# Merge weights of three attention groups: one set for both halves, and by token for the last head pair

## The chip, the cores and the metric

The kernel runs on one core of a Trainium2 chip. The metric is the device time of one execution in microseconds. The engines that matter here are TensorE (PE, and PEld for its weight loads), VectorE (DVE), ScalarE (ACT), GpSimd (POOL) and the queue of SyncE (SP), which issues nearly all DMAs.

## What is computed

The reference is a two-layer decoder trunk of 1024 tokens with width 1024: layer one has a forgetting attention and a gated ConvFFN, layer two a dilated attention with three groups of heads ("mixer B") and again a ConvFFN. The change lies in mixer B, where the outputs of the three groups are merged by softmax weights over their log-sum-exp:

```
for g, (window, dil) in enumerate(B_GROUPS):          # (128,1), (512,4), (2048,16)
    o_g, lse_g = dilated_branch(q[:, :, g], kv[:, :, 0, g], kv[:, :, 1, g], dil, slopes[g])
    outs.append(o_g)
    lses.append(lse_g)
alpha = softmax(stack(lses, axis=0), axis=0)
o = sum(alpha[..., None] * stack(outs, axis=0), axis=0)
x = x + o.reshape(B, S, B_OUT_WIDTH) @ b_w_out[bl]
```

There are 8 heads of 64 in each group, and each head has one weight per token and group.

## The kernel before

Matrix products are made of float32r pairs: each operand is split into a high part (ACT, `split` L152) and a low part (DVE, L153), and three matmuls (L116, L117, L118) stand for one product.

Mixer B works on 12 units: 4 head pairs p, and for each the groups g = 2, 1, 0 in this order. A unit's attention (`attend_b`) goes through two halves m of the tokens and two heads j; after both heads of a half it calls `each_half(m)`. While a unit attends, the projections of the next unit (values, queries, keys) are woven in as filler by `weave`. The last unit (p = 3, g = 0) has as filler the first half of the output projection (`out_proj(b_w_out[0], 0, xT)`), which may begin once the last pair's first half is placed in `yh` and `yl`. All instructions are then put in order by a scheduler with a timeline of its own: each engine's and each queue's order is fixed at build time, and an engine whose next instruction waits does not go past it.

The softmax leaves, for each token, head and group, the minimum (k = 0) and the sum (k = 1) in a tile `st` with tokens on the partitions. `spread` transposes a group's 32 columns on PE (L534), copies them out on ACT into the one-buffer tile `srow` (L537, L539) and sends them to DRAM (`stat_sp[p]`) in token order: for g = 0 in rows of 512 bytes (L543), for g = 1 in four DMAs of single 4-byte elements, 8 rows of 128 elements each (L548), for g = 2 in eight DMAs of 8-byte pieces (L554).

`group_weights` is called once per half. It loads the half's stats on 32 partitions with 32 tokens each (two DMAs, L563, tile `stats`), makes the three weights in 12 small DVE instructions and one Exp on ACT (L567 to L577), writes them to DRAM (L578, tile `wt`), and reads them back spread over 64 partitions per head (two DMAs, L581, tile `wb` of two buffers, 128 x 3 x 512). `merge_b` multiplies the groups' outputs `og` by them (L589: g = 2 and 1 on the given engine, g = 0 on DVE) and adds (L590, L591). `emit_o` splits the result and sends it to DRAM (`o_sp`, tiles `oh` and `ol` with one buffer each), or, for the last pair, splits it straight into `yh` and `yl`.

For the pairs 0 to 2 this is done in the next pair's g = 2 unit: the weights of both halves at `each_half(0)`, the products and sums at `each_half(1)` with POOL for g = 2 and 1. The tiles of `group_weights` have one buffer, so the second half's loads come after the first half's stats have been read. For the last pair, `each_half(m)` in its own g = 0 unit spreads that half's g = 0 stats, makes the weights and merges on DVE at once. Ahead of that unit `reload` brings back, half by half, the earlier pairs' outputs into `yh` and `yl` (L614, L615) and the residual into `xT` (L617).

Of the kernel before, what the change touches and what calls it, by code (L numbers as in the profile page):

```python
# [8 lines left out]
F32 = mybir.dt.float32  # L9
# [3 lines left out]
ALU = mybir.AluOpType  # L13
# [3 lines left out]
P = 128  # L17
# [33 lines left out]
def trunk(ctx, tc, x, a_w_in, a_b_f, a_w_out, b_w_q, b_w_out, kv_norm_g, w_kv,  # L51
# [478 lines left out]
    def spread(ap, psc, st, g, dst, ms=(0, 1)):  # L530

        n = 16 * len(ms)
        tp = psc.tile([P, H2], F32, name="sc")
        nc.tensor.transpose(tp[:n, :P], st[:, g, 16 * ms[0]:16 * ms[0] + n], ident)  # L534
        rows = ap.tile([32, P], F32, name="srow")
# [5 lines left out]
        if g == 0:  # L541
            for i, m in enumerate(ms):
                nc.sync.dma_start(dst[0, m].rearrange("k j (b t) -> (k j b) t", t=P),  # L543
                                  rows[16 * i:16 * i + 16])
# [13 lines left out]
    def group_weights(ap, src, dst, m):  # L558

        T = 32  # L560
        r = ap.tile([32, NG, 2, T], F32, name="stats")
        for k in range(2):
            nc.sync.dma_start(r[:, :, k], src[:, m, k].rearrange("g j (b t) -> (j b) g t", t=T))  # L563
        mn, sm = (ap.tile([32, T], F32, name=n) for n in ("mn", "sm"))
        e = ap.tile([32, NG, T], F32, name="ew")
        el = r[:, :, 1]
        nc.vector.tensor_tensor(out=mn, in0=r[:, 0, 0], in1=r[:, 1, 0], op=ALU.min)  # L567
        nc.vector.tensor_tensor(out=mn, in0=mn, in1=r[:, 2, 0], op=ALU.min)
        for g in range(NG):
            nc.vector.tensor_tensor(out=e[:, g], in0=r[:, g, 0], in1=mn, op=ALU.subtract)  # L570
        nc.scalar.activation(e, e, AF.Exp, scale=-1.0)
        nc.vector.tensor_tensor(out=el, in0=e, in1=el, op=ALU.mult)
        nc.vector.tensor_tensor(out=sm, in0=el[:, 0], in1=el[:, 1], op=ALU.add)
        nc.vector.tensor_tensor(out=sm, in0=sm, in1=el[:, 2], op=ALU.add)
# [3 lines left out]
        nc.sync.dma_start(dst[m].rearrange("g j (b t) -> (j b) g t", t=T), e)  # L578
        w = ap.tile([P, NG, H2], F32, name="wb", bufs=2)
        for j in range(2):  # L580
            nc.sync.dma_start(w[64 * j:64 * j + 64],  # L581
                              dst[m][:, j].unsqueeze(0).to_broadcast([64, NG, H2]))
        return w
# [782 lines left out]
```

## Time and profile before

| what | value |
|---|---|
| median of 3 runs | 2688.72 us (2683.15 to 2688.9) |
| profiled execution | 2687.51 us, of which the span is 2685.7 us |
| mean granted TensorE clock | 0.984 |
| PE busy | 2576.5 us (96% of the span) |
| DVE busy | 1953.0 us (73%) |
| ACT busy | 1334.9 us (50%) |
| POOL busy | 546.7 us (20%) |

The profiled execution is the one that all rows below come from, and a sum over its rows is made against its own 2687.51 us; what is outside its span is 1.8 us. Mixer B's attention takes the stretch from about 1380 to 1940 us of the span; the merges of the pairs 0, 1 and 2 fall around 1500 to 1535, 1640 to 1675 and 1780 to 1815 us, and that of the last pair into 1893 to 1940 us. In a windows row the columns give, for one stretch, the busy time of each engine with the number of its instructions, the granted TensorE clock as a share of its full speed, the DMA engines' busy share and what they moved. In a timeline row the bracket at the end says how long the engine stood idle before and what ended that.

### The profile page before, as it was taken

How to read it: one execution, taken by the hardware profiler on the slowest of the kernel's cores; microseconds unless marked ns; L12 is line 12 of the kernel's file. 1: busy time of each engine (PE TensorE's matmuls, PEld its weight loads, DVE VectorE, ACT ScalarE, POOL GpSimd, SP SyncE). 2: the span in 40 equal slices, each digit the busy share in tenths (PEclk: the TensorE clock that was granted, in tenths of full speed). 3: DMA queues.
4: the chain of work that ended last, by engine and by line, in shares of the span. 5: the costliest groups of instructions: out<-in, count | busy, mean ns of one | idle time of the engine just before them, and what ended most of it. 6: DMA issues, size and time to landing. Idle time of an engine off the chain costs nothing.

```text
span 2685.7 us, 36967 instructions
## 1 busy us (share of the span) xinstructions
PE 2576.5 (96%) x12734; PEld 2148.6 (80%) x12734; DVE 1953.0 (73%) x3859; ACT 1334.9 (50%) x2832; POOL 546.7 (20%) x629
## 2 busy tenths in 40 slices
PE   7999999999999999999899999999589999999998
PEld 5998888787788888888688787878467888888887
DVE  6677777767876777788866766666588777777787
ACT  6566555654544443444455555555345444443444
POOL 0222222310121121121132223231011221111121
PEclk9999999999999999999899999999799999999999
DMA  5122112532111111111413222233421111111113
GB/s 185 48 65 57 49 50 71 184 89 83 48 48 55 52 59 54 49 51 51 136 40 40 69 32 73 37 73 95 111 88 43 52 48 55 51 59 55 48 48 114
DMA packets 282467, 182.12 MB, mean 68 GB/s; under 512 B 40480, under 2 KB 259368, under 8 KB 282280
## 3 DMA queue, kind: packets, MB, share of 16 engines
q1 hardware_dynamic: 282168, 179.75, 24.2%
q8 instruction: 100, 1.64, 0.2%
q14 instruction: 87, 0.71, 0.1%
q10 hardware_dynamic: 112, 0.02, 0.0%
HBM read 151.55 MB, written 23.98 MB: 65 GB/s over the span
## 4 chain that ended last, share of the span: by engine, by line
PE 82%; DVE 9%; DMA 4%; ACT 3%; issue 2%; POOL 0%; SPq 0%; POOLq 0%; ACTq 0%; DVEq 0%
PE up L781 29%; PE mm L116 13%; PE mm L117 13%; PE mm L118 13%; PE po L247 4%; PE tp L234 3%; DVE u L732 1%; DVE t L257 1%; PE sc L357 1%; DMA wb<-wt 1%; PE sc L358 1%; PE up L116 1%; PE up L118 1%; PE up L117 1%; DVE pt L153 1%
## 5 line engine op out<-in xcount | busy, mean ns | idle before, releaser
L116 PE MATMUL mm<-yh,wh 128*128 128x512 f32 x960 | 383.7, 400 | 12.0 <-ACT yh L152 7.3
L117 PE MATMUL mm<-yl,wh 128*128 128x512 f32 x960 | 382.7, 399 | 3.9 <-DVE yl L153 3.4
L118 PE MATMUL mm<-yh,wl 128*128 128x512 f32 x960 | 380.6, 396 | 0.0
L152 ACT CAST wh<-wraw 128x512 fp32r<-128x512 f32 x228 | 140.8, 619 | 356.5 <-PE up L781 306.6
L886 DVE TENSOR_TENSOR xT<-mm,xT 128x512 f32<-128x512 f32 x320 | 217.8, 684 | 107.0 <-PE mm L118 105.3
L153 DVE TENSOR_TENSOR wl<-wraw,wh 128x512 fp32r<-128x512 f32 x228 | 169.4, 748 | 150.3 <-ACT wh L152 150.3
L781 PE MATMUL up<-yh,wh 128*128 128x512 f32 x704 | 274.4, 390 | 0.9 <-ACT wh L152 0.9
L781 PE MATMUL up<-yl,wh 128*128 128x512 f32 x704 | 274.1, 389 | 0.0
L781 PE MATMUL up<-yh,wl 128*128 128x512 f32 x704 | 268.9, 389 | 0.0
L117 PE MATMUL mm<-ml,wh 128*128 128x512 f32 x576 | 225.4, 391 | 1.4 <-DVE ml L153 1.4
L116 PE MATMUL mm<-mh,wh 128*128 128x512 f32 x576 | 224.7, 390 | 0.0
L118 PE MATMUL mm<-mh,wl 128*128 128x512 f32 x576 | 223.9, 389 | 0.0
L116 PEld LDWEIGHTS mm<-yh,wh 128*128 128x128 f32 x960 | 182.4, 190 | 51.4 <-ACT yh L152 7.9
L247 PE MATMUL po<-pt,v 128*128 128x256 f32 x1040 | 195.6, 294 | 19.8 <-DVE pt L153 14.7
L117 PEld LDWEIGHTS mm<-yl,wh 128*128 128x128 f32 x960 | 182.6, 190 | 37.3 <-DVE yl L153 4.1
L118 PEld LDWEIGHTS mm<-yh,wl 128*128 128x128 f32 x960 | 182.4, 190 | 34.6
L152 ACT CAST pt<-tp 128x128 fp32r<-128x128 f32 (+2 forms) x408 | 149.6, 382 | 104.6 <-PE tp L234 57.7
L153 DVE TENSOR_TENSOR pt<-tp,pt 128x128 fp32r<-128x128 f32 (+2 forms) x408 | 169.4, 432 | 44.0 <-ACT pt L152 39.3
L247 PEld LDWEIGHTS po<-pt,v 128*128 128x128 f32 x1040 | 156.8, 192 | 39.6 <-DVE pt L153 19.1
L765 POOL TENSOR_TENSOR sraw<-fraw 128x512 f32<-128x512 f32 x40 | 68.3, 1709 | 580.0 <-DMA fraw<-in_ffn_w_up_dram 314.4
L95 DVE TENSOR_TENSOR wl<-wraw,wh 128x512 fp32r<-128x512 f32 x176 | 127.0, 724 | 75.1 <-ACT wh L94 66.2
L781 PEld LDWEIGHTS up<-yh,wh 128*128 128x128 f32 x704 | 132.2, 188 | 29.8 <-ACT wh L152 1.8
(346 smaller groups left out, 6086.9 us busy)
## 6 DMA issues: line engine op xcount, KB each, us to landing
wraw<-in_ffn_w_down_dram SPq DMA_DIRECT2D x104, 256.0 KB
fraw<-in_ffn_w_up_dram SPq DMA_DIRECT2D x88, 256.0 KB
wraw<-in_ffn_w_up_dram SPq DMA_DIRECT2D x88, 256.0 KB
wraw<-in_a_w_in_dram SPq DMA_DIRECT2D x60, 256.0 KB
wraw<-in_w_kv_dram SPq DMA_DIRECT2D x48, 256.0 KB
wraw<-in_a_w_out_dram SPq DMA_DIRECT2D x32, 256.0 KB
xT<-x_sp SPq DMA_DIRECT2D x32, 256.0 KB
wraw<-in_b_w_q_dram SPq DMA_DIRECT2D x24, 256.0 KB
```

The lines of the kernel that those rows point to most:

```text
L95: nc.vector.tensor_tensor(out=wl, in0=raw, in1=wh.bitcast(F32), op=ALU.subtract)
L116: nc.tensor.matmul(ps, ah, bh, start=(i == 0), stop=False)
L117: nc.tensor.matmul(ps, ah, bl, start=False, stop=False)
L118: nc.tensor.matmul(ps, al, bh, start=False, stop=(i == n - 1))
L152: nc.scalar.copy(h, src)
L153: return nc.vector.tensor_tensor(out=l, in0=src, in1=h.bitcast(F32), op=ALU.subtract).ins
L234: nc.tensor.transpose(tp[:, i * P:(i + 1) * P], c, ident)
L247: nc.tensor.matmul(po[:, col:col + 2 * P], v(kb), pt[:, hl, i * 2 * P:(i + 1) * 2 * P], start=(first and i == 0 and hl == 0), stop=(last a ...
L257: nc.vector.tensor_tensor_reduce(out=t[:, a:b], in0=sc, in1=m, scale=1.0, scalar=INIT if ci == 0 else nm[ci - 1], op0=ALU.add, op1=ALU.min ...
L765: nc.gpsimd.tensor_tensor(out=raw[n], in0=raw[a], in1=raw[b], op=op)
L781: nc.tensor.matmul(ps[bank], a[:, c], b[:, k], start=(start and k == 0 and i == 0), stop=(k == KH - 1 and i == 2), skip_group_check=True)
L886: nc.vector.tensor_tensor(out=xT[:, d, sl], in0=ps, in1=xT[:, d, sl], op=ALU.add)
```

## The change

Pairs 0 to 2: `group_weights` takes both halves at once. It loads their stats on 64 partitions (four DMAs), makes the weights once (`weigh`, which has 14 DVE instructions, and one Exp), writes them with two DMAs, and issues all four loads of the two `wb` tiles one behind the other. The products stay where they were in the program, in `each_half(1)`.

Last pair: the g = 0 stats are no longer spread. `stats_by_token` loads the stats of g = 1 and 2 back with tokens on the partitions, four DMAs in the order (g, m) = (1, 0), (1, 1), (2, 0), (2, 1), each of 128 partitions with 16 single 4-byte elements; it stands in the program behind `reload`. `last_weights` makes the weights of a half from them and from `st` on 128 partitions x 8 (`weigh`), and for each group copies them on ACT into a 128 x 512 tile in which each weight stands 64 times, transposes that with four PE transposes into a PSUM bank of `psc` (three banks in all), and `merge_b` reads the weights from there.

`spread` for g = 0 of the other pairs is one DMA in place of two.

```
-    def group_weights(ap, src, dst, m):
-        r = ap.tile([32, NG, 2, T], F32, name="stats")
-        for k in range(2):
-            nc.sync.dma_start(r[:, :, k], src[:, m, k].rearrange("g j (b t) -> (j b) g t", t=T))
...
-        nc.sync.dma_start(dst[m].rearrange("g j (b t) -> (j b) g t", t=T), e)
-        w = ap.tile([P, NG, H2], F32, name="wb", bufs=2)
-        for j in range(2):
-            nc.sync.dma_start(w[64 * j:64 * j + 64],
-                              dst[m][:, j].unsqueeze(0).to_broadcast([64, NG, H2]))
-        return w
+    def weigh(e, nms, ls, mn, sm):
+        nc.vector.tensor_tensor(out=mn, in0=nms[0], in1=nms[1], op=ALU.min)
+        nc.vector.tensor_tensor(out=mn, in0=mn, in1=nms[2], op=ALU.min)
         for g in range(NG):
+            nc.vector.tensor_tensor(out=e[:, g], in0=nms[g], in1=mn, op=ALU.subtract)
         nc.scalar.activation(e, e, AF.Exp, scale=-1.0)
+        for g in range(NG):
+            nc.vector.tensor_tensor(out=mn if g else sm, in0=e[:, g], in1=ls[g], op=ALU.mult)
+            if g:
+                nc.vector.tensor_tensor(out=sm, in0=sm, in1=mn, op=ALU.add)
         nc.vector.reciprocal(sm, sm)
         for g in range(NG):
             nc.vector.tensor_tensor(out=e[:, g], in0=e[:, g], in1=sm, op=ALU.mult)
+    def group_weights(ap, src, dst):
+        r = ap.tile([P, NG, 2, T], F32, name="stats")[:64]
+        for m in range(2):
+            for k in range(2):
+                nc.sync.dma_start(r[32 * m:32 * m + 32, :, k],
+                                  src[:, m, k].rearrange("g j (b t) -> (j b) g t", t=T))
...
+        weigh(e, [r[:, g, 0] for g in range(NG)], [r[:, g, 1] for g in range(NG)], mn, sm)
+        for m in range(2):
+            nc.sync.dma_start(dst[m].rearrange("g j (b t) -> (j b) g t", t=T),
+                              e[32 * m:32 * m + 32])
+        ws = []
+        for m in range(2):
+            w = ap.tile([P, NG, H2], F32, name="wb", bufs=2)
+            for j in range(2):
+                nc.sync.dma_start(w[64 * j:64 * j + 64],
+                                  dst[m][:, j].unsqueeze(0).to_broadcast([64, NG, H2]))
+            ws.append([w[:, g] for g in range(NG)])
+        return ws
+    def stats_by_token(ap, src):
+        r = ap.tile([P, NG, 2, 32], F32, name="stats")[:, :, :, :16]
+        for g in (1, 2):
+            for m in range(2):
+                nc.sync.dma_start(r[:, g, m].rearrange("t (a b) -> t a b", b=4),
+                                  src[g, m].rearrange("k j (b t) -> t (k j) b", t=P))
+        return r
+    def last_weights(ap, psc, st, r, m):
+        mn, sm = (ap.tile([P, 32], F32, name=n)[:, :8] for n in ("mn", "sm"))
+        e = ap.tile([P, NG, 32], F32, name="ew")[:, :, :8]
+        spare = ap.tile([P, NG, H2], F32, name="wb", bufs=2)
+        own = [st[:, 0, 16 * m:16 * m + 16]] + [r[:, g, m] for g in (1, 2)]
+        weigh(e, [t[:, :8] for t in own], [t[:, 8:] for t in own], mn, sm)
+        ws = []
+        for g in range(NG):
+            tp = psc.tile([P, H2], F32, name="sc")
+            lx = spare[:, g].rearrange("p (b j d) -> p b j d", b=4, j=2)
+            nc.scalar.copy(lx, e[:, g].rearrange("p (j b) -> p b j", j=2).unsqueeze(3)
+                           .to_broadcast([P, 4, 2, 64]))
+            for b in range(4):
+                nc.tensor.transpose(tp[:, b * P:(b + 1) * P],
+                                    lx[:, b].rearrange("p j d -> p (j d)"), ident)
+            ws.append(tp)
+        return ws
...
             def each_half(m):
                 if last:
-                    spread(ap, psc, st, 0, stat_sp[p], (m,))
-                    out_half(p, ogs, group_weights(ap, stat_sp[p], wt_sp[p], m), m, nc.vector)
+                    out_half(p, ogs, last_weights(ap, psc, st, by_token, m), m, nc.vector)
                     return
...
                     if m == 0:
-                        ws += [group_weights(ap, stat_sp[pp], wt_sp[pp], hf) for hf in range(2)]
+                        ws += group_weights(ap, stat_sp[pp], wt_sp[pp])
...
                 reload(xT, p)
                 placed.clear()
                 filler = out_proj(b_w_out[0], 0, xT)
+                by_token = stats_by_token(ap, stat_sp[p])
```

## Rows read from the trace of the kernel before

**Rows 1.** The page's first part: busy time, share and instructions of TensorE.

```profile
PE 2576.5 (96%) x12734; PEld 2148.6 (80%) x12734; DVE 1953.0 (73%) x3859; ACT 1334.9 (50%) x2832; POOL 546.7 (20%) x629
```

**Rows 2.** Windows by stage: between merges, merge of pair 0, last pair.

```profile
1400.00:1490.00 90.00, 90.00 (x488) 77.42 (x487) 58.15 (x145) 53.52 (x145) 21.27 (x35) 1.00 0.29 39
1490.00:1540.00 50.00, 44.02 (x229) 36.79 (x228) 36.06 (x101) 21.95 (x70) 15.57 (x22) 0.97 0.29 77
...
1880.00:1945.00 65.00, 36.38 (x162) 27.75 (x161) 37.99 (x108) 25.62 (x74) 2.62 (x8) 0.71 0.48 108
```

**Rows 3.** Windows around the second half's products of the pairs 0, 1 and 2.

```profile
1526.00:1534.00 8.00, 4.20 (x17) 3.44 (x16) 4.70 (x10) 0.94 (x3) 4.86 (x5) 0.79 0.28 79
1667.00:1674.00 7.00, 4.14 (x15) 3.29 (x14) 2.62 (x6) 0.00 (x0) 4.80 (x5) 0.76 0.32 87
1808.00:1811.00 3.00, 0.82 (x7) 0.58 (x6) 0.89 (x2) 0.00 (x0) 1.12 (x1) 1.00 0.72 197
```

**Rows 4.** Timeline of DVE: g = 0 products, both of pair 0, second of pair 2.

```profile
1511.94 1.23 DVE L589 TENSOR_TENSOR og<-og,wb 128x512 f32<-128x512 f32 x1
...
1528.34 1.80 DVE L589 TENSOR_TENSOR og<-og,wb 128x512 f32<-128x512 f32 x1 [3.60 <-DMA wb<-wt]
...
1809.87 0.69 DVE L589 TENSOR_TENSOR og<-og,wb 128x512 f32<-128x512 f32 x1 [3.09 <-DMA wb<-wt]
```

**Rows 5.** Timeline of SP's queue: both halves' weights of pair 0.

```profile
1503.11 0.36 SPq L578 DMA_DIRECT2D wt<-ew  x1
...
1504.79 1.34 SPq L581 DMA_DIRECT2D wb<-wt  x2
...
1521.59 1.24 SPq L581 DMA_DIRECT2D wb<-wt  x2
```

**Rows 6.** Timeline of POOL: the first half's two products of pair 0.

```profile
1511.33 2.98 POOL L589 TENSOR_TENSOR og<-og,wb 128x512 f32<-128x512 f32 x2 [3.59 <-DMA wb<-wt]
```

**Rows 7.** Tile stats: its DVE and DMA forms, duration minimum, median, maximum in ns.

```profile
L570 DVE TENSOR_TENSOR ew<-stats,mn x24: 171/174/180, 1500.6 to 1918.1; 32x32 f32<-32x32 f32 x24
```

**Rows 8.** Timeline of DVE, last pair: first stats, first and second half's products, placing.

```profile
1911.96 0.18 DVE L567 TENSOR_TENSOR mn<-stats 32x32 f32<-32x32 f32 x1 [12.02 <-DMA stats<-stat]
...
1917.85 0.38 DVE L570 TENSOR_TENSOR ew<-stats,mn 32x32 f32<-32x32 f32 x3 [0.71 <-DMA wt<-ew]
...
1920.15 0.37 DVE L577 TENSOR_TENSOR ew<-ew,sm 32x32 f32<-32x32 f32 x3
...
1932.34 0.76 DVE L153 TENSOR_TENSOR yl<-og,yh 128x256 fp32r<-128x256 f32 x2
```

**Rows 9.** Timeline of PE, last pair: attention's transposes, output projection's start.

```profile
1913.43 0.90 PE L234 MATMUL tp<-ident,t 128*128 128x128 f32 x3 [11.60 <-DVE pt L153]
...
1933.16 0.79 PE L117 MATMUL mm<-yl,wh 128*128 128x512 f32 x1 [3.42 <-DVE yl L153]
```

**Rows 10.** Timeline of SP's queue: four-byte stores of two pairs, reload of xT.

```profile
1449.39 6.04 SPq L548 DMA_DIRECT2D stat<-srow  x4
...
1875.86 10.90 SPq L548 DMA_DIRECT2D stat<-srow  x4
...
1896.22 7.66 SPq L617 DMA_DIRECT2D xT<-x_sp  x8
```

**Rows 11.** Timeline of ACT: the copy that waits until the four-byte stores have landed.

```profile
1897.04 0.25 ACT L537 COPY srow<-sc 16x128 f32<-16x128 f32 x1 [1.88 <-DMA stat<-srow]
```

**Rows 12.** Chain of waits: stats' load for pair 0, last pair's DMAs.

```profile
1498.00 1.65 DMA stats<-stat
...
1905.59 4.79 DMA stat<-srow
...
1920.59 3.43 DMA wt<-ew
...
1924.71 5.49 DMA wb<-wt
```

**Rows 13.** Groups of ACT from 1890 to 1940 us, shapes apart.

```profile
L152 ACT CAST pt<-tp 128x512 fp32r<-128x512 f32 x4 | 2.3, 577 | 0.8 <-PE tp L234 0.8
```

More of the change, by code (lines that the diff above doesn't have):

```diff
@@ L528, in stat, with spread @@
         return st[:, g, c:c + 1]
-    def spread(ap, psc, st, g, dst, ms=(0, 1)):
-        n = 16 * len(ms)
+    def spread(ap, psc, st, g, dst):
+        n = 32
         tp = psc.tile([P, H2], F32, name="sc")
-        nc.tensor.transpose(tp[:n, :P], st[:, g, 16 * ms[0]:16 * ms[0] + n], ident)
-        rows = ap.tile([32, P], F32, name="srow")
+        nc.tensor.transpose(tp[:n, :P], st[:, g], ident)
+        rows = ap.tile([n, P], F32, name="srow")
         if g < 2:
@@ L541, in spread @@
         if g == 0:
-            for i, m in enumerate(ms):
-                nc.sync.dma_start(dst[0, m].rearrange("k j (b t) -> (k j b) t", t=P),
-                                  rows[16 * i:16 * i + 16])
+            nc.sync.dma_start(dst[0].rearrange("m k j (b t) -> (m k j b) t", t=P), rows)
         elif g == 1:
@@ L556, in spread @@
                             rows[i:i + 8, 64 * m:64 * m + 64].rearrange("b (l h) -> b l h", h=2))
-    def group_weights(ap, src, dst, m):
-        T = 32
-        r = ap.tile([32, NG, 2, T], F32, name="stats")
-        for k in range(2):
-            nc.sync.dma_start(r[:, :, k], src[:, m, k].rearrange("g j (b t) -> (j b) g t", t=T))
[L564 to L568, printed above, removed]
+    def weigh(e, nms, ls, mn, sm):
+        nc.vector.tensor_tensor(out=mn, in0=nms[0], in1=nms[1], op=ALU.min)
+        nc.vector.tensor_tensor(out=mn, in0=mn, in1=nms[2], op=ALU.min)
         for g in range(NG):
-            nc.vector.tensor_tensor(out=e[:, g], in0=r[:, g, 0], in1=mn, op=ALU.subtract)
+            nc.vector.tensor_tensor(out=e[:, g], in0=nms[g], in1=mn, op=ALU.subtract)
         nc.scalar.activation(e, e, AF.Exp, scale=-1.0)
-        nc.vector.tensor_tensor(out=el, in0=e, in1=el, op=ALU.mult)
-        nc.vector.tensor_tensor(out=sm, in0=el[:, 0], in1=el[:, 1], op=ALU.add)
-        nc.vector.tensor_tensor(out=sm, in0=sm, in1=el[:, 2], op=ALU.add)
+        for g in range(NG):
+            nc.vector.tensor_tensor(out=mn if g else sm, in0=e[:, g], in1=ls[g], op=ALU.mult)
+            if g:
+                nc.vector.tensor_tensor(out=sm, in0=sm, in1=mn, op=ALU.add)
         nc.vector.reciprocal(sm, sm)
@@ L577, in group_weights @@
             nc.vector.tensor_tensor(out=e[:, g], in0=e[:, g], in1=sm, op=ALU.mult)
-        nc.sync.dma_start(dst[m].rearrange("g j (b t) -> (j b) g t", t=T), e)
-        w = ap.tile([P, NG, H2], F32, name="wb", bufs=2)
-        for j in range(2):
-            nc.sync.dma_start(w[64 * j:64 * j + 64],
-                              dst[m][:, j].unsqueeze(0).to_broadcast([64, NG, H2]))
-        return w
+    def group_weights(ap, src, dst):
+        T = 32
+        r = ap.tile([P, NG, 2, T], F32, name="stats")[:64]
[3 more added lines that the diff above has]
+                                  src[:, m, k].rearrange("g j (b t) -> (j b) g t", t=T))
+        mn, sm = (ap.tile([P, T], F32, name=n)[:64] for n in ("mn", "sm"))
+        e = ap.tile([P, NG, T], F32, name="ew")[:64]
+        weigh(e, [r[:, g, 0] for g in range(NG)], [r[:, g, 1] for g in range(NG)], mn, sm)
[10 more added lines that the diff above has]
+        return ws
@@ L588, in merge_b @@
         for g in (2, 1, 0):
-            (eng if g else nc.vector).tensor_tensor(out=o[g], in0=o[g], in1=w[:, g], op=ALU.mult)
+            (eng if g else nc.vector).tensor_tensor(out=o[g], in0=o[g], in1=w[g], op=ALU.mult)
         nc.vector.tensor_tensor(out=o[1], in0=o[1], in1=o[2], op=ALU.add)
```

## The prediction

> **What bounds the kernel now.** I read the page's first part, windows by stage, the timelines of the stalls, and the chain of waits. TensorE is busy for 96% of the span [rows 1]: time is gained only where it stands idle or runs at its lower clock. The windows by stage say where that is in mixer B. Between merges it is busy for all 90 of 90 us. In the 50 us around pair 0's merge it is busy for 44.02, and in the 65 us of the last pair's merge for 36.38, at a mean granted clock of 0.71 [rows 2]; pairs 1 and 2 look like pair 0. So the change touches the places that have something to give: roughly 5 us at each of three merges, and 29 us at the last one.
>
> **The stall in pairs 0 to 2.** DVE reaches the second half's product and waits 3.60 us (pair 0) and 3.09 us (pair 2) for `wb` [rows 4]; pair 1 is alike. The queue says why: the first half's weights went out at 1503.11 and their read-back at 1504.79, but the second half's read-back is issued only at 1521.59 [rows 5], because its weights come from tiles with one buffer and sit behind other work on DVE. While DVE stands, nothing splits the transposed probabilities and PE runs dry. In the windows around the three second products PE lacks 8.00 - 4.20 = 3.80, 7.00 - 4.14 = 2.86 and 3.00 - 0.82 = 2.18 us, 8.84 together; the granted clock falls to a mean of 0.79 and 0.76 in the first two, after PE's idle stretch, which costs 8 x 0.21 + 7 x 0.24 = 3.4 us more [rows 3]. Upper bound of the gain: 12.2 us.
>
> **What the first edit does there.** Both halves' weights come from one chain. DVE loses 2 x 12 small instructions and gets 14: 10 x 0.174 us [rows 7] = 1.7 us less for each pair, in a stage where DVE is crowded. The queue has two more loads of stats before the chain, some 0.4 us each by their issue, and one more store of weights: the first half's read-back goes out about 1 us later. The second half's read-back follows at once, some 17 us earlier than 1521.59; it queues behind the first one's transfer, so it lands about 2 x 1.34 us of issue later, and far ahead of where its product stood. The stall above goes. What is late next is the first half's product. It had 1511.94 - 1511.33 = 0.6 us in hand (POOL began as soon as the weights had landed, after a wait of 3.59 us) [rows 4, 6]. The read-back is 1 us later, and DVE arrives over 1 us earlier because the second chain no longer stands ahead: it now waits some 1.5 to 2 us. Also, both halves' products may now follow each other, with four results through the one-buffer `oh` and `ol`; each reuse waits for a store. Lower bound of the gain: 0, if these short waits cost PE as much as the long one; a loss would need them longer than the one removed, and nothing was put ahead of the first read-back but three short DMAs. But a wait of 3.1 to 3.7 us cost 2.2 to 3.8 us of PE, and a shorter one meets more queued matmuls. I let a third of the 12 us stay: **-8 us**.
>
> **The last pair now.** DVE stands 12.02 us until the first half's stats come back, at 1911.96 [rows 8]. They were late because the g = 0 stores, ready when ACT copied the stats at 1897.04 [rows 11], stood on SP's queue behind the reload of `xT`, 1896.22 to 1903.9 [rows 10], went out at 1905.59 and took 4.79 us [rows 12]. Then follow weights, store, read-back (3.43 and 5.49 us for the second half [rows 12]) and products; `yl` is split at 1932.34 [rows 8] and the output projection starts at 1933.16 [rows 9]. It is 21.2 us from the stats to the start.
>
> **What the second edit does there.** The path becomes: stats by token, weights, spread by PE, products. Call T the time when the by-token loads have landed.
> - From T on there are 14 DVE instructions and one Exp. The ten of them from the subtractions to the last weights took 1917.85 to 1920.52 = 2.7 us with the Exp [rows 8]; four more at 0.174 [rows 7] make 3.4 us. Then three ACT copies of 128 x 512 at 0.58 [rows 13] = 1.7, and four transposes behind the last copy: three took 0.90 at the low clock [rows 9], so 1.2. The first product, g = 2, takes the bank made last, so no product starts earlier; three products and two sums at 0.69 [rows 4] make 3.4. ACT and DVE split 256 columns, two on DVE in 0.76 [rows 8], one of them on the path: 0.8. Sum 10.5, and 1.5 for attention work that stands between them in DVE's order: T + 12. All three banks of `psc` are held from the copies to the products; the last unit's scores are done by then, as PE has only transposes and value products left after 1913 [rows 9]; without that cover the scores would wait some 5 us.
> - The ACT copy of the g = 0 stats goes too, with its 1.88 us of waiting [rows 11]: inside the same stretch, not counted again.
> - T itself. The loads of g = 1 depend on the stores L548 of the unit before, which landed at 1897.0 [rows 11], whatever place on the queue they get. Each load has 128 x 16 = 2048 runs of four bytes. No such load is in the trace; the nearest rows are L548's stores of 1024 four-byte runs. Quiet: four in 6.04 us of issue [rows 10] = 1.47 ns for a run, 3.0 us for a load. Loaded, from 1875.86 until landed at 1897.04 [rows 10, 11]: 21.2 us for 4096 = 5.2 ns, 10.6 us for a load. The first half needs three of the four loads. With 1.6 us to land [rows 12], T lies between 1897 + 9.0 + 1.6 = 1907.6 and 1897 + 31.8 + 1.6 = 1930.4. I take 2 ns, near the quiet row, since at 1897 only the reload competes and a load has no store's way to DRAM: 1897 + 12.3 + 1.6 = 1910.9.
> - Start of the projection: 1910.9 + 12 = 1922.9 against 1933.2: **-10 us**. Between the bounds: -13.6 to +9.2.
> - The reload of the second half (`yh`, `yl`, `xT`) and two loads of the output weights stand behind the by-token loads on SP if these come first. They are wanted by the second half's projection, more than 20 us after the first one's start, which hides up to 12 us of delay.
>
> The DMA row bears on a rule that speaks against this edit. The trace shows that L548's issue alone takes 1.5 to 2.7 us each [rows 10], where each of eight reload DMAs of 256 KB has 0.96 with its waits. The Trainium skill, "DMA: Bandwidth & Descriptors", section "Rules for kernel authors", says that a last dimension that isn't contiguous becomes one descriptor per element and should be rearranged; the trace agrees. By its section "Bandwidth" a packet costs about 10.5 ns at the smallest sizes, by which three loads would need an estimated 64.5 us and the edit would lose about 42 us; the stores here took 1.5 to 5.2 ns, so I don't go by it.
>
> **Sum.** 2687.5 - 8 - 10 = **2669.5 us**. The profiled execution lies 1.2 us under the median of the runs shown, so I forecast for it as for them.
>
> **Rivals.**
> - *The wait only moves* in pairs 0 to 2: the four read-backs share the DMA engines and DVE waits at the first product for as long as it did at the second. For it: only 0.6 us in hand. Against: two more transfers of the same size are behind, not ahead. Then 2687.5 - 10 = 2677.5.
> - *The by-token loads go out behind the reload.* They stand behind it in the program, and the order is the scheduler's. Then they start at 1903.9: T = 1917.8, start 1929.8, -3.4 in place of -10: 2676.
> - *The by-token loads run at the loaded pace*, 5.2 ns, and the weights wait for three: start 1942.4, +9.2 - 8: 2688.7, no change.
> - *Slower:* the same pace, and the first weights wait for all four loads (one tile, one wait): T = 1897 + 42.4 + 1.6 = 1941, start 1953, +19.8 - 8: 2699. It decides from the point where the start lies 13.4 us behind 1933.2, that is T = 1934.6: four loads at over 4.4 ns a run. For it: DVE's order is fixed, so the rest of the attention stands behind the weights, and the loads do share the engines with the reload. Against: the quiet stores, and that a load has no write to DRAM. The page's rule above names just this form of transfer; it is this rival that it would make likely.
>
> **How the numbers follow.** Forecast 0.45, moved wait 0.18, loads behind the reload 0.15, loaded pace with three 0.08, with four 0.14. A measurement here tells 0.2%, 5.4 us, from no change. The first three are faster almost wholly, with some of the third within the bound: faster 0.70; the fourth and the edges of the others are the same: 0.14; the fifth is slower, with a little of the fourth: 0.16. The range: low end 2687.5 - 12.2 - 13.6 - 6 = 2655, all of the stall gone, the loads at the quiet pace, and the stores before them landed 6 us earlier because the reload stands behind them (half of the 10.9 us of their issue [rows 10], an estimate); high end 2690, which takes in the loaded pace with three loads and leaves out the slower case. The forecast's own range is 2658 to 2680.
>
> **What would show it.** In the profile after: no wait of DVE for `wb` at the second product of pairs 0 to 2, a wait under 2 us at the first, and PE's clock at 1.00 around it; the queue with four read-backs in a row. In the last pair: the by-token loads between 1897 and 1912, DVE's wait ending by about 1911, the projection's start near 1923. The prediction is wrong if DVE stands at the first weights until after 1920, or if the stall in front of the products is as long as before.

## The result, and the profile after

| | before | after |
|---|---|---|
| median | 2688.44 us (2683.15 to 2688.9, 4 runs) | 2670.77 us (2669.12 to 2674.17, 4 runs) |
| span of the profiled execution | 2685.7 us | 2672.3 us |
| mean granted TensorE clock | 0.984 | 0.985 |

The ratio is 0.994, with a 95% interval from 0.9923 to 0.9958: 17.7 us faster by the medians. The forecast was 2669.5.

A single profiled execution doesn't place this gain well, because the part of the program up to the first of the marks below takes 1404 to 1410 us in the executions of this study, with nothing changed there. So I cut the span at two marks on SP's queue: the g = 2 stats stores of pair 0 and of pair 3. Between them lie the merges of the pairs 0 to 2 (stage A); from the second to the end lie the last pair and all that follows (stage B). Timeline of SP, before:

```profile
1405.58 3.15 SPq L554 DMA_DIRECT2D stat<-srow  x8
...
1828.53 3.12 SPq L554 DMA_DIRECT2D stat<-srow  x8
```

The same marks after (here L554 is still the line of these stores):

```profile
1407.08 3.15 SPq L554 DMA_DIRECT2D stat<-srow  x8
...
1825.37 3.13 SPq L554 DMA_DIRECT2D stat<-srow  x8
```

Stage A took 1828.53 - 1405.58 = 422.95 us before and 418.29 after: 4.7 us less. Stage B took 2685.7 - 1828.53 = 857.2 and 2672.3 - 1825.37 = 846.9: 10.2 us less. The front (up to the first mark) was 1.5 us longer in this execution of after, which is why the spans differ by 13.4 only. Windows between the marks, before and after (stretch, its length, PE busy with the number of its instructions first, granted clock third from the end):

```profile
1405.58:1828.53 422.95, 408.56 (x2179) 346.97 (x2177) 282.81 (x742) 232.22 (x651) 112.61 (x169) 0.99 0.29 54
...
1407.08:1825.37 418.29, 409.21 (x2179) 347.06 (x2178) 283.77 (x714) 231.40 (x649) 113.59 (x169) 0.99 0.28 54
```

PE has the same 2179 instructions in both. What got shorter is its idle time: 422.95 - 408.56 = 14.4 us before, 9.1 after.

**Pairs 0 to 2.** The queue of pair 0 after: the stats' loads, then, behind the weights' store, four read-backs in a row, where [rows 5] had the second half's 17 us later.

```profile
1499.63 1.73 SPq L579 DMA_DIRECT2D stats<-stat  x4
...
1509.98 2.68 SPq L591 DMA_DIRECT2D wb<-wt  x4
```

DVE's timeline for the same merge, the products (L628), the sum of g = 1 and 2 (L629) and the reuse of `ol`:

```profile
1516.37 0.69 DVE L628 TENSOR_TENSOR og<-og,wb 128x512 f32<-128x512 f32 x1 [2.30 <-DMA wb<-wt]
1519.49 0.69 DVE L629 TENSOR_TENSOR og<-og,og 128x512 f32<-128x512 f32 x1 [2.43 <-POOL og L628]
...
1526.61 0.68 DVE L628 TENSOR_TENSOR og<-og,wb 128x512 f32<-128x512 f32 x1
...
1531.45 0.98 DVE L153 TENSOR_TENSOR ol<-og,oh 128x256 fp32r<-128x256 f32 x1 [1.59 <-DMA o_sp<-ol]
```

The wait at the second product, 3.60 us in [rows 4], is gone. A wait of 2.30 us stands at the first product, which had none, and one of 2.43 behind it, because POOL can begin its two products only when the same weights have landed. In the pairs 1 and 2 the first wait is 0.93 and 1.22, the second 2.43 and 2.44. The tile `wb` counts them all; before:

```profile
  DVE og L589: 15.4, 5
  DVE og L590: 5.4, 3
```

After:

```profile
  DVE og L629: 7.3, 3
  DVE og L628: 5.7, 4
```

Without the last pair's share, DVE waited at the products 3.60 + 3.74 + 3.09 = 10.4 us before and 2.30 + 0.93 + 1.22 = 4.5 after, and for POOL 5.4 and 7.3: in all 15.8 and 11.8. But `ol` lost those 4 us again: its waits for its one buffer grew from three to six. The tile `ol`, before and after:

```profile
  DMA o_sp<-ol: 3.3, 3
```

```profile
  DMA o_sp<-ol: 7.4, 6
```

All these waits together are 19.1 us before and after alike, so their sum does not explain the 4.7 us of stage A; PE's idle time does, 5.3 us less. How much of it each wait costs PE is not shown. PE's clock did not get better around pair 0, where [rows 2] had 0.97:

```profile
1490.00:1540.00 50.00, 47.27 (x239) 39.17 (x238) 34.22 (x88) 22.86 (x69) 16.25 (x23) 0.93 0.31 82
```

**Last pair.** SP's queue after:

```profile
1835.39 2.35 SPq L601 DMA_DIRECT2D stats<-stat  x2
...
1870.17 9.84 SPq L548 DMA_DIRECT2D stat<-srow  x4
1880.06 5.22 SPq L656 DMA_DIRECT2D xT<-x_sp  x3
...
1894.87 5.47 SPq L656 DMA_DIRECT2D xT<-x_sp  x8
1900.68 4.50 SPq L601 DMA_DIRECT2D stats<-stat  x2
```

The two by-token loads of g = 2 went out long ahead; those of g = 1 stand behind the whole reload. DVE's timeline, the first weights and the placing of the first half:

```profile
1906.38 0.17 DVE L560 TENSOR_TENSOR mn<-st,stats 128x8 f32<-128x8 f32 x1 [17.03 <-DMA stats<-stat]
...
1912.36 0.32 DVE L571 TENSOR_TENSOR ew<-ew,sm 128x8 f32<-128x8 f32 x3
...
1921.86 0.75 DVE L153 TENSOR_TENSOR yl<-og,yh 128x256 fp32r<-128x256 f32 x2
```

PE's timeline:

```profile
1907.28 1.77 PE L247 MATMUL po<-pt,v 128*128 128x256 f32 x3 [16.80 <-DVE pt L153]
...
1922.11 0.73 PE L116 MATMUL mm<-yh,wh 128*128 128x512 f32 x2 [0.28 <-ACT yh L152]
...
1922.82 0.39 PE L117 MATMUL mm<-yl,wh 128*128 128x512 f32 x1
```

DVE's stall is longer than before (17.03 against 12.02 us [rows 8]) and still the path is shorter: from the stats to the projection's first product with `yl` (L117) it takes 1922.82 - 1906.38 = 16.4 us, where it took 21.2. From the second mark, that product comes after 1922.82 - 1825.37 = 97.5 us, before after 1933.16 - 1828.53 = 104.6 [rows 9]: 7.2 earlier.

The 1933.16 of [rows 9] is not the projection's first instruction before. PE had begun with `yh` (L116) at 1928.51 and then stood 3.42 us for `yl`. In DVE's order two of the second half's products stood ahead of the split of `yl`, and the first of them waited 2.92 us for its own weights. PE and DVE before:

```profile
1928.51 1.22 PE L116 MATMUL mm<-yh,wh 128*128 128x512 f32 x2 [1.40 <-ACT yh L152]
```

```profile
1930.29 1.29 DVE L589 TENSOR_TENSOR og<-og,wb 128x512 f32<-128x512 f32 x2 [2.92 <-DMA wb<-wt]
```

The first product with `yh` comes 1922.11 - 1825.37 = 96.7 us from the mark after and 1928.51 - 1828.53 = 100.0 before, only 3.2 earlier. So 3.9 of the 7.2 us come from the gap between the two, 4.65 us before and 0.71 after: the second half no longer stands between `yh` and `yl` of the first. Windows of after:

```profile
1894.00:1914.00 20.00, 6.14 (x22) 4.80 (x22) 6.06 (x28) 4.76 (x15) 0.62 (x2) 0.50 0.79 237
...
1923.00:1945.00 22.00, 22.00 (x108) 18.47 (x108) 18.25 (x40) 11.07 (x22) 0.00 (x0) 1.00 0.37 108
```

And of before, behind the first product with `yl`:

```profile
1934.00:1945.00 11.00, 9.43 (x29) 6.71 (x29) 6.67 (x13) 5.24 (x11) 0.00 (x0) 0.73 0.35 98
```

In the 22 us from 1923 on PE runs without a gap at a mean granted clock of 1.00 (2.4 GHz) after; before it had 9.43 of 11 us at 0.73. Stage B gained 3 us more than the 7.2 of the earlier product; they may lie here, but no run separates them.

### The profile page after: what moved, and what is told of

It reads as the page before. It is cut to its first block, busy times and chain, and to the rows that moved or that the text cites. A ratio compares the mean times of both kernels' runs of the same rounds, so it can differ in the third digit from the quotient of the medians.

```text
span 2672.3 us, 36987 instructions
## 1 busy us (share of the span) xinstructions
PE 2578.6 (96%) x12756; PEld 2150.4 (80%) x12756; DVE 1951.5 (73%) x3833; ACT 1336.6 (50%) x2833; POOL 552.0 (21%) x629
## 4 chain that ended last, share of the span: by engine, by line
PE 83%; DVE 8%; DMA 4%; ACT 3%; issue 2%; SPq 1%; POOL 1%; POOLq 0%; ACTq 0%; DVEq 0%
PE up L820 30%; PE mm L116 13%; PE mm L117 13%; PE mm L118 13%; PE po L247 4%; PE tp L234 3%; DVE u L771 1%; DVE t L257 1%; PE sc L357 1%; PE sc L358 1%; PE up L116 1%; PE up L117 1%; PE up L118 1%; PE sc L477 1%; DMA wb<-wt 1%
## 5 line engine op out<-in xcount | busy, mean ns | idle before, releaser
L116 PE MATMUL mm<-yh,wh 128*128 128x512 f32 x960 | 381.3, 398 | 9.0 <-ACT yh L152 6.2
L117 PE MATMUL mm<-yl,wh 128*128 128x512 f32 x960 | 381.8, 398 | 1.2 <-DMA yl<-o_sp 1.2
L153 DVE TENSOR_TENSOR wl<-wraw,wh 128x512 fp32r<-128x512 f32 x228 | 167.9, 742 | 152.0 <-ACT wh L152 151.9
L117 PE MATMUL mm<-ml,wh 128*128 128x512 f32 x576 | 225.4, 391 | 1.5 <-DVE ml L153 1.5
L116 PE MATMUL mm<-mh,wh 128*128 128x512 f32 x576 | 224.8, 390 | 0.0
L116 PEld LDWEIGHTS mm<-yh,wh 128*128 128x128 f32 x960 | 181.5, 189 | 45.5 <-ACT yh L152 6.7
L247 PE MATMUL po<-pt,v 128*128 128x256 f32 x1040 | 196.2, 294 | 20.3 <-DVE pt L153 18.6
L117 PEld LDWEIGHTS mm<-yl,wh 128*128 128x128 f32 x960 | 181.9, 189 | 34.0 <-DMA yl<-o_sp 1.4
L95 DVE TENSOR_TENSOR wl<-wraw,wh 128x512 fp32r<-128x512 f32 x176 | 134.3, 766 | 67.4 <-ACT wh L94 61.8
```

What stands on the lines that cost most here:

```text
L95: nc.vector.tensor_tensor(out=wl, in0=raw, in1=wh.bitcast(F32), op=ALU.subtract)
L116: nc.tensor.matmul(ps, ah, bh, start=(i == 0), stop=False)
L117: nc.tensor.matmul(ps, ah, bl, start=False, stop=False)
L153: return nc.vector.tensor_tensor(out=l, in0=src, in1=h.bitcast(F32), op=ALU.subtract).ins
L247: nc.tensor.matmul(po[:, col:col + 2 * P], v(kb), pt[:, hl, i * 2 * P:(i + 1) * 2 * P], start=(first and i == 0 and hl == 0), stop=(last a ...
```

## The experiments

The theory at this point: two independent gains, about 4 us in stage A and 10 to 13 in the last pair. What is left has a cause in each: in the last pair the place on the queue (theory P) or the single elements (rival S); in the pairs 0 to 2 the place of the products in DVE's order, ahead of their weights (theory W), or simply DVE's load (rival L). The runs were made in four batches, each beside runs of the kernel before on the same chip (medians 2687.24 to 2689.72):

| run | median us | ratio, 95% interval | A us | B us |
|---|---|---|---|---|
| before | 2688.44 | | 422.95 | 857.2 |
| after | 2670.77 | 0.994 [0.9923, 0.9958] | 418.29 | 846.9 |
| e1_pairs_only | 2684.43 | 0.9987 [0.9979, 0.9996] | 419.15 | 856.6 |
| e2_token_only | 2674.88 | 0.9952 [0.994, 0.9965] | 422.05 | 846.0 |
| e3_loads_first | 2664.93 | 0.9918 [0.9904, 0.9931] | 420.00 | 837.2 |
| e5_packed_first | 2655.38 | 0.9878 [0.9863, 0.9893] | 418.82 | 827.2 |
| e4_packed | 2655.01 | 0.9877 [0.9862, 0.9892] | 418.68 | 829.8 |
| e11_one_store | 2656.56 | 0.9884 [0.9868, 0.9901] | 418.59 | 830.6 |
| e6_other_factor | 2663.12 | 0.9911 [0.9896, 0.9927] | 404.13 | 851.7 |
| e7_pool_less | 2668.74 | 0.993 [0.9917, 0.9942] | 414.41 | 846.9 |
| e9_packed_pool_less | 2655.15 | 0.9877 [0.9864, 0.9891] | 414.87 | 830.7 |
| e10_tokens_all | 2654.84 | 0.9879 [0.986, 0.9898] | 414.40 | 830.0 |
| e12_late_04 | 2641.76 | 0.9824 [0.9811, 0.9837] | 406.69 | 828.9 |
| e12_late_06 | 2639.44 | 0.9816 [0.9803, 0.9829] | 407.77 | 824.8 |

A is one execution, yet the six kernels that merge the pairs 0 to 2 alike (after, e1, e3, e5, e4, e11) lie between 418.29 and 420.00. So 3 us in A tell something; in B it takes more (827.2 to 830.7 in e5, e4, e9 and e10, with the same last pair). The marks stand in the queue's order, and a new order can move them against PE's work: these six have 2179 to 2185 PE instructions between the marks. Where a count differs by more, I reckon 0.19 us for an instruction (408.56 us for 2179).

**Each edit alone.** e1 keeps `group_weights` for both halves and the old last pair (its diff is against after); e2 keeps the old pairs 0 to 2 and has the new last pair (against before).

```
e1:  def each_half(m):
         if last:
+            spread(ap, psc, st, 0, stat_sp[p], (m,))
+            out_half(p, ogs, half_weights(ap, stat_sp[p], wt_sp[p], m), m, nc.vector)
...
e2:  def each_half(m):
         if last:
-            spread(ap, psc, st, 0, stat_sp[p], (m,))
-            out_half(p, ogs, group_weights(ap, stat_sp[p], wt_sp[p], m), m, nc.vector)
+            out_half(p, ogs, last_weights(ap, psc, st, by_token, m), m, nc.vector)
```

> First edit alone: pairs 0 to 2 as in the changed kernel, the last pair as before. The prediction's theory (the second wait goes, two thirds of the idle time and the clock come back): 8 us faster than before, ratio 0.997. Rival (what the windows of the changed kernel show: TensorE has only some 5.6 us more busy time around the three merges, and the first product has a new wait of 2.3 us): 3 to 5 us faster, ratio 0.998 to 0.999, within what can be told from no change.

> Second edit alone: the pairs 0 to 2 as before, the last pair by token. The prediction's theory: 10 us faster than before, ratio 0.9963. Rival (nearly the whole gain is here, as the output projection starts about 11 us earlier and TensorE runs at the full clock from then): 12 to 14 us faster, ratio 0.995. If the two edits add up, this and the run with the first edit alone give 17.7 us together.

Measured: 3.6 us for the first (2688.0 - 2684.4), 13.1 for the second (2688.0 - 2674.9). Together 16.7, against 17.7 for both: they add up. The rival was right on both. The stages say the same: e1 moves A by 3.8 and B by 0.5, e2 A by 0.9 and B by 11.2.

**Place on the queue.** e3 puts the by-token loads ahead of the reload.

```
+                by_token = stats_by_token(ap, stat_sp[p])
                 reload(xT, p)
                 placed.clear()
                 filler = out_proj(b_w_out[0], 0, xT)
-                by_token = stats_by_token(ap, stat_sp[p])
```

> The changed kernel with the by-token loads ahead of the reload in the program; on the queue the two loads of g = 1 then stand before the second half of the reload instead of behind it. Theory (VectorE's wait of 17.0 us is the place on the queue): the loads go out about 1887 and have landed by 1895 instead of 1906.4, VectorE waits 5 to 7 us, the projection starts 9 to 11 us earlier, 8 to 10 us faster than the changed kernel, ratio to before 0.990 to 0.991. Rival (single elements set it: the stores of g = 1 land late, and the loads take 5 us more whatever their place): landed at 1903 or later, at most 3 us faster than the changed kernel, ratio 0.993 to 0.994.

SP's queue in e3:

```profile
1872.80 9.82 SPq L548 DMA_DIRECT2D stat<-srow  x4
1882.66 5.22 SPq L656 DMA_DIRECT2D xT<-x_sp  x3
1894.44 3.37 SPq L601 DMA_DIRECT2D stats<-stat  x2
```

DVE in e3:

```profile
1898.98 0.17 DVE L560 TENSOR_TENSOR mn<-st,stats 128x8 f32<-128x8 f32 x1 [6.91 <-DMA stats<-stat]
```

Both had a part. The wait falls from 17.03 to 6.91, so 10 us of it were the place. But the loads, next on the queue at 1887.9, went out at 1894.44: they wait for the four stores of single elements, whose last issue had ended 11.8 us earlier, at 1882.62. That is the late landing that the rival named. B falls by 9.8, the time by 5.8, less than the 8 to 10 expected.

**Single elements.** e5 and e4 store the row of g = 1 in one DMA, reordered by ACT's copy so that four weights of a token lie together, and load runs of 16 bytes; e5 with the loads first, e4 behind the reload. e11 is e4 without the reordering: one store, but the loads are of 4 bytes again.

```
+        if packed:
+            nc.scalar.copy(rows.rearrange("n (i b) -> n i b", b=4),
+                           tp[:n, :P].rearrange("n (b i) -> n i b", b=4))
+            nc.sync.dma_start(dst[1].rearrange("m k j (x t) -> (m k j x) t", t=P), rows)
+            return
...
+        for q in range(4):
+            nc.sync.dma_start(r[q::4, 1, 0].rearrange("t (n b) -> t n b", b=4), v[q])
```

> As the run with the loads first, and the g = 1 stats of the last pair are stored in one DMA of 32 rows of 512 bytes (reordered in the copy out of PSUM) and loaded in four DMAs of 256 runs of 16 bytes each, in place of 4096 single elements each way. Theory of the queue's place: little beyond the loads first, 1 to 3 us. Rival (single elements set it): the 9.84 us that the four stores hold the queue and the 4.50 us of the loads shrink to about 0.4 and 1.6 us, the stats have landed before VectorE wants them (about 1889), its wait is under 2 us; start of the projection near 1906, 14 to 16 us faster than the changed kernel, ratio to before 0.988 to 0.989.

> The g = 1 stats of the last pair in one store of 32 x 512 bytes and four loads of 16-byte runs, as in the run that was both packed and first, but with the loads behind the reload in the program, as in the changed kernel. Theory (the single-element stores are the root: they hold the queue 9.84 us, land about 12 us after that, and the reload crawls meanwhile; the place behind the reload costs little once they are gone): the reload is out by 1884, the loads follow and land by about 1889, VectorE's wait is under 2 us, and the time is that of packed and first within 2 us, 13 to 15 us under the changed kernel, ratio to before 0.988 to 0.989. Rival (the two add up: 5.8 us for the place, 9.6 for the elements): 9 to 10 us under the changed kernel, ratio 0.990 to 0.991.

> As the packed kernel with the loads behind the reload, on the same queue order, but the row is not reordered before its one store, so the loads of g = 1 are of single 4-byte elements again: four DMAs of 1024 runs each, the same 4096 runs as in the changed kernel. Theory (the single-element stores were the root, the loads by token are cheap): the loads take 3 to 6 us of issue from about 1885 and have landed by 1893, VectorE waits 0 to 2 us, the time within 2 us of the packed kernel, ratio to before 0.9875 to 0.989. Rival (single elements cost as much when loaded): the loads land at 1898 or later, VectorE waits 5 us or more, 4 to 8 us above the packed kernel, ratio 0.989 to 0.991.

SP's queue in e4:

```profile
1872.84 0.33 SPq L541 DMA_DIRECT2D stat<-srow  x1
1873.45 1.60 SPq L664 DMA_DIRECT2D xT<-x_sp  x3
...
1879.79 4.73 SPq L664 DMA_DIRECT2D xT<-x_sp  x8
```

e5 is 15.4 us under after, as S forecast and P did not. In e4 the reload takes 1884.52 - 1873.45 = 11.1 us, in after 1900.34 - 1880.06 = 20.3, the same DMAs in the same order. DVE waits for nothing at the first weights, in e4 and e5 alike, and their times are equal (2655.01 and 2655.38). DVE in e4, then in e5:

```profile
1892.54 0.16 DVE L565 TENSOR_TENSOR mn<-st,stats 128x8 f32<-128x8 f32 x1
```

```profile
1889.41 0.16 DVE L565 TENSOR_TENSOR mn<-st,stats 128x8 f32<-128x8 f32 x1
```

So the place costs nothing once the single-element stores are gone: they were the root (rival S), and the place hurt because they had made the reload late. e11 tells stores from loads. SP and DVE in e11:

```profile
1880.50 6.36 SPq L606 DMA_DIRECT2D stats<-stat  x4
```

```profile
1889.14 0.17 DVE L564 TENSOR_TENSOR mn<-st,stats 128x8 f32<-128x8 f32 x1 [0.99 <-DMA stats<-stat]
```

4096 single elements loaded took 6.36 us of issue and cost DVE 0.99 us; the time is the packed kernel's within what can be told. Stored, as many held the queue for 9.84 us and made everything behind them late.

**POOL's share of the products.** e7 is after, e9 is e5, with

```
-            (eng if g else nc.vector).tensor_tensor(out=o[g], in0=o[g], in1=w[g], op=ALU.mult)
+            (eng if g == 2 else nc.vector).tensor_tensor(out=o[g], in0=o[g], in1=w[g], op=ALU.mult)
```

> The changed kernel, but in the pairs 0 to 2 POOL makes only the g = 2 product and VectorE those of g = 1 and 0. Theory of the moved wait: the sum's wait for POOL, 2.4 us at each pair, falls under 0.5, VectorE gets 2 x 0.7 us of work more for each pair; 1 to 2 us faster than the changed kernel, ratio to before 0.993 to 0.9935. Rival (VectorE is full there): the added 4.2 us of work cost as much as the waits, no faster or up to 2 us slower, ratio 0.994 to 0.995.

> Packed and first for the last pair, and POOL with the g = 2 product alone in the pairs 0 to 2. By the theory of the moved wait 1 to 2 us under the packed and first kernel, about 2654, ratio to before 0.987 to 0.9875; by the rival at its time or up to 2 us above it, 0.988 to 0.9885.

DVE in e7: the sum follows the products without a wait.

```profile
1514.67 2.39 DVE L628 TENSOR_TENSOR og<-og,wb 128x512 f32<-128x512 f32 x2 [2.40 <-DMA wb<-wt]
1516.99 0.68 DVE L629 TENSOR_TENSOR og<-og,og 128x512 f32<-128x512 f32 x1
```

A falls by 3.9 us in both, although DVE has 4.2 us more to do: for W. The time falls by 2.0 in e7 and by 0.2 in e9, which is at the edge of what times can tell here: the gain is seen in the stage alone.

**No wait for the weights.** e6 takes a constant as factor in the pairs 0 to 2. It leaves the weights out of the products there; they are still made, stored and read back.

```
+            t, u = o[g], w[g]
+            if eng is nc.gpsimd:
+                t = t.rearrange("p (b t) -> p b t", t=P)
+                u = ident.unsqueeze(1).to_broadcast([P, 4, P])
```

> The changed kernel, but in the pairs 0 to 2 the products read a constant tile of the same shape in place of the weights (the weights are still made, stored and read back, and not used). So nothing there waits for the read-back. Theory (in the pairs 0 to 2 most of the gain went into the new wait at the first product, 2.3, 0.9 and 1.2 us, and the wait for POOL behind it, 2.4 us each): VectorE's two waits are gone, TensorE's idle stretch behind them too, 3 to 5 us faster than the changed kernel, ratio to before 0.992 to 0.993. Rival (VectorE is simply full in that stretch, and the work of the merge costs TensorE the same wherever its waits are): within 1 us of the changed kernel, ratio 0.9935 to 0.994.

7.6 us faster than after, twice the forecast, and A is 14.2 shorter: PE is busy for all of the window that had 47.27 of 50 in after.

```profile
1490.00:1540.00 50.00, 50.00 (x272) 42.77 (x271) 35.95 (x103) 28.87 (x87) 14.57 (x22) 1.00 0.35 82
```

But this run does more than take a wait away. Its order is another: the first half's products moved ahead into a stretch where nothing was short. And B is 4.8 us longer. Most of that is the second mark, which stands earlier in PE's work than in after:

```profile
1404.00:1808.13 404.13, 400.10 (x2162) 340.65 (x2161) 278.20 (x709) 229.34 (x645) 114.86 (x167) 1.00 0.31 56
```

17 instructions fewer than the 2179 of after are 3.2 us of work that B has in place of A; the stage's own gain is nearer to 11 us, and 1.6 us of B stay without a cause. The run shows that the merge's waits and its place cost several us; it doesn't say how to get them.

**Weights earlier.** e10 makes the weights of every pair by token, straight from `st` for g = 0, and transposes them once; the round trip of the g = 0 stats through DRAM is gone. It also stores the g = 1 stats of every pair in one DMA, as e5 does for the last.

```
-                    spread(ap, psc, st, g, stat_sp[p], i == len(units) - 2)
-                    if g == 0:
-                        due.append((p, ogs, []))
+                    if g:
+                        spread(ap, psc, st, g, stat_sp[p], g == 1)
+                    else:
+                        r = stats_by_token(ap, stat_sp[p])
+                        due.append((p, ogs, pair_weights(ap, psc, st, r, wt_sp[p])))
```

> A candidate to beat both: the g = 1 stats packed for every pair, the weights of the pairs 0 to 2 made by token from the stats tile itself and from the loads by token, transposed once by TensorE, stored in one DMA and read back spread as before. The g = 0 stats no longer go through DRAM, so the read-back of the weights can start one round trip earlier (the changed kernel: store at 1497.1, loads at 1499.6, landed about 1501.7). Theory of the moved wait: the weights land some 4 us earlier, VectorE's wait at the first product, 0.9 to 2.3 us, is gone in all three pairs, the wait for POOL stays at 2.4 us only where VectorE gets there early; 3 to 5 us under the packed and first kernel, about 2651, ratio to before 0.986 to 0.987. Rival (the merge's place and VectorE's load cost TensorE the same): within 1.5 us of the packed and first kernel, ratio 0.9875 to 0.988.

The read-back goes out 1505.29 - 1408.79 = 96.5 us from the first mark, in after 1509.98 - 1407.08 = 102.9. DVE, at the first product of pair 0:

```profile
1511.52 0.69 DVE L652 TENSOR_TENSOR og<-og,wb 128x512 f32<-128x512 f32 x1 [1.57 <-DMA wb<-wt]
```

It still waits, and in the pairs 1 and 2 for 2.02 and 3.07 us, longer than in after. The order had moved the product earlier along with its weights: to 1511.52 - 1408.79 = 102.7 us from the mark, from 109.3 in after. A falls by 4.4 against e5, but B is 2.8 longer and the time falls by 0.5: no gain that the time can tell. To bring a transfer forward brought little here, since the order brought its consumer forward as well.

**Products later.** e12 leaves the transfers alone and ties DVE's products to a later softmax, on top of e9: that of block 6, or in e12_late_04 of block 4. A zero made from that softmax's statistics is added to one column of the outputs, so the products can't stand ahead of it.

```
+        if behind is not None:
+            z = ap.tile([P, 1], F32, name="z")
+            nc.vector.tensor_tensor(out=z, in0=behind, in1=behind, op=ALU.subtract)
+            for g in (0, 1):
+                nc.vector.tensor_tensor(out=o[g][:, :1], in0=o[g][:, :1], in1=z, op=ALU.add)
...
+                                    stat(st, 2, 1, 0, 6))
```

> Packed and first, POOL with the g = 2 product alone, and in the pairs 0 to 2 VectorE's products are tied to a later point of its order: a zero made from the statistics of the softmax of block 6 of the second half (head 0) is added to one column of the outputs of g = 0 and 1, so that the products stand behind that softmax. That is three very short VectorE instructions more for each half; the values don't change. The weights' way is as before. Theory (the order puts the products where the weights have not yet landed, and VectorE stands while softmaxes that TensorE wants are queued behind): VectorE comes to the first product some 3 to 4 us later, with that work done, its wait for the weights there is under 0.5 us (1.8 to 2.5 us without the tie), TensorE has 4 to 6 us more in the three windows; 3 to 6 us under packed and first, ratio to before 0.9855 to 0.987. Rival (what is left there is VectorE's load, not its wait): no faster, ratio 0.9875 to 0.988.

> The same with the products tied to block 4, two softmaxes earlier. Theory: VectorE's wait for the weights at the first product is shorter than without the tie and longer than with block 6, 0 to 1 us; 2 to 5 us under packed and first, ratio to before 0.986 to 0.987. Rival: no faster, 0.9875 to 0.988.

The marks on SP's queue, e12_late_06:

```profile
1403.85 3.15 SPq L559 DMA_DIRECT2D stat<-srow  x8
...
1811.62 1.92 SPq L559 DMA_DIRECT2D stat<-srow  x4
```

DVE at the first products of pair 0:

```profile
1523.79 1.28 DVE L641 TENSOR_TENSOR og<-og,wb 128x512 f32<-128x512 f32 x2
1526.50 0.68 DVE L642 TENSOR_TENSOR og<-og,og 128x512 f32<-128x512 f32 x1
```

In the three pairs no product and no sum of DVE waits for the weights or for POOL's product any more. From the first mark the products come at 1523.79 - 1403.85 = 119.9 us, in after at 1516.37 - 1407.08 = 109.3, 10.6 us later, and the stage is shorter for it: A falls by 7.1 us (e12_late_06) and 8.2 (e12_late_04) against e9, B by 5.9 and 1.8. Here too the second mark has moved, the other way. Between the marks, e9 and e12_late_06:

```profile
1410.32:1825.19 414.87, 406.91 (x2178) 343.72 (x2177) 283.24 (x718) 231.51 (x647) 106.13 (x163) 1.00 0.30 55
```

```profile
1403.85:1811.62 407.77, 404.79 (x2196) 346.59 (x2195) 283.27 (x739) 234.23 (x651) 103.84 (x164) 1.00 0.30 55
```

With 18 instructions more, and 7 more in e12_late_04 (2185), the stage's own gain is nearer to 10.5 and 9.5 us, and 2.5 and 0.5 of B remain. PE's idle time between the marks falls from 8.0 to 3.0 us; why its instructions are shorter on the average as well is open. The time falls by 15.7 and 13.4, far more than the 3 to 6 and 2 to 5 expected; what A and B leave of it lies within the scatter of the fronts (1403.85 to 1410.32). The order around the products moved with them, so the runs show what the later place is worth with all that follows from it. e12_late_06, 2639.44 us, is the best kernel of the study: 50 us or 1.84% under before (its own comparison), 31 under after. What is late next in pair 0 stands on POOL:

```profile
1516.70 1.27 POOL L641 TENSOR_TENSOR og<-og,wb 128x512 f32<-128x512 f32 x1 [2.09 <-DMA wb<-wt]
1517.91 0.52 POOL L241 MEMSET pt<- 128x512 f32 x1
1518.52 0.30 POOL L466 TENSOR_SCALAR bias<-dist 128x128 f32<-128x128 f32 x1
```

POOL still waits for the weights, and the memset and the bias queued behind it hold PE for 1.42 us and DVE for 1.92.

## Why the prediction came out right, point by point

- **The time** is right (2670.8 for 2669.5, inside the forecast's own range), and the last pair's term is near: B fell by 10.2, e2's time by 13.1, for the forecast's 10. The term of the pairs 0 to 2 was too large: 3.6 us by e1's time, 4.7 by stage A, for 8. By e1 and e2 one term was 4.4 too large and the other 3.1 too small; that the sum came within 1.3 us is in part luck.
- **The step that failed: "I let a third of the 12 us stay".** The waits themselves were foreseen: the second product's is gone, the first product's is 2.30, 0.93 and 1.22 for "some 1.5 to 2", and `ol` waits for its store (1.59 and 0.85 us in pair 0). Too small was what they cost together: POOL's two products now begin with the weights, so the sum stands 2.43 us in each pair (before 0.96 to 2.21, behind the second product), and `ol` waits 4.1 us more in all. The clock of 1.00 around the merge did not come in pair 0: it was 0.93. With the second wait the reason for the first went unasked: the order puts the product where the weights have not yet landed. e10 and e12 show that it is the place in the order, and e7 that POOL's share is part of it. The rival "the wait only moves" named the mechanism; its size, nothing gained, was too hard.
- **"Upper bound of the gain: 12.2 us"** bounds the stall at the second products alone, and for it the clock is charged too high: 8 x 0.21 and 7 x 0.24 count the lower clock also for the 3.80 and 2.86 us in which PE did nothing. It does not bound the stage: e12 cut A by 15.2 and 16.3 us from before, with the products in a later place and one of POOL's given to DVE.
- **T.** Forecast 1910.9, which is 82.4 us after the second mark; measured 1906.38 - 1825.37 = 81.0. Right by compensation. "The first half needs three of the four loads" was wrong: g = 2's pair had gone at 1835.39, and only two were still to come. "1897" as their start was wrong too: they went behind the reload, as a rival had it, 75.3 us from the second mark for its 75.4. And they were quicker than 2 ns a run: 4.50 us of issue for 4096.
- **"At 1897 only the reload competes and a load has no store's way to DRAM"** led to the quiet pace, and that was right: 4.50 us of issue in after, 6.36 in e11. Why loads are quick, no run shows. The loaded pace and the slower rival built on it found no support.
- **T + 12** came out as 16.4, to the first product with `yl`. The scores were not "done by then": the weights stand in DVE's order ahead of the last unit's softmaxes and splits, which then come between. To the last weights it took 6.3 us (1912.36 + 0.32 - 1906.38) for 3.4, and from there to that product 10.1 (1922.82 - 1912.68) for 7.1; the forecast had 1.5 for attention work in both together.
- **"-10"** for the earlier start was 7.2 by the product that the forecast took for the start, and 3.2 by the projection's first. "21.2 us from the stats to the start" was misread: it holds the second half's products and their wait of 2.92 us, which stood ahead of `yl`. That they left the path is worth 3.9 of the 7.2, and the forecast did not name it. The rest of B's gain may lie in a PE without gaps at the clock of 1.00 afterwards, which it had not counted.
- **The rule on single elements** was weighed with the right rows and half the right answer. The price by which three loads would have needed 64.5 us did not come. The Trainium skill, "DMA: Bandwidth & Descriptors", section "Rules for kernel authors", asks to rearrange a last dimension that isn't contiguous. For the stores it pays: B falls by 16 to 20 us (e4, e5, e11). For the loads it doesn't, in e11 against e4 (830.6 and 829.8).

## What to carry to other kernels

When a wait is removed, look for the next thing in the same order: who else waits for the same transfer, and what stands behind it on each engine; an engine that takes its instructions in order pays for a product that is placed ahead of its operand, and here placing it later was worth more (e12) than fetching the operand sooner (e10). Cut the span at marks in the queue on both sides of a change, since a stage of 420 us repeats to 2 us where the whole varies by 6, and count PE's instructions between them, since a mark can move too. Price the stores that a load depends on, and what they do to the transfers behind them, not only the load.

## What the runs showed of the hardware

- Four DMAs that store 1024 single 4-byte elements each hold SP's queue for 9.82 us ahead of the last unit (6.04 for pair 0 of the same run), and a load that depends on them starts 11.8 us after the last issue has ended (e3). Four that load as many take 6.36 us of issue and were waited for 0.99 us (e11). One store of 32 rows of 512 bytes takes 0.33 us of issue (e4).
- Behind such stores the same 17 reload DMAs take 20.3 us to issue, without them 11.1.
- PE stood for 16.80 us behind DVE's stall, until 1907.28. From 1894 to 1914 us its mean granted clock was 0.50 (1.2 GHz), with 6.14 of 20 us busy; from 1923 to 1945, without gaps, it was 1.00 (2.4 GHz).
